# Letting token mixers in between the row tiles of the last layer's gate and branch products

## The chip, the core and the metric

One core of one Trainium2 chip runs the whole program, two layers of a trunk, as one launch. The metric is the device time of that launch in microseconds, the median of several runs. All times below are microseconds from the start of the span unless something else is said.

## What is computed

The reference is a two-layer trunk over 256 latent tokens and 256 context tokens of width 1024. In each layer one input projection feeds four mixers (a convolution module, a bidirectional state-space scan, a bidirectional retention, and a latent attention). What the mixers give is merged like this:

```
merged = sigmoid(gate_0) * (branch_0 @ w_branch[0])
for i in 1..3: merged += sigmoid(gate_i) * (branch_i @ w_branch[i])
out = merged @ w_out
```

Here gate_i is a 1024-wide part of the input projection `hx @ w_in`, and each branch is 512 wide. Then come an output projection with a residual, a norm and a SwiGLU. In the last layer only the 256 latent tokens go on, so the context tokens need no gates and no branch products there.

The convolution branch, the one that matters most below, is a 31-tap depthwise convolution, a layer norm over its 512 channels, and a SiLU.

## The kernel before, in words

All large products are made from a stream of weights: 128x128 blocks, eight to a chunk of 512 KB. Each chunk is loaded on the queue of SyncE, and then split into two parts, a rounded one (`whi`, one cast on ScalarE, L201) and the rest (`wlo`, two subtractions on VectorE, L268). A product of two such split operands is three matmuls (`mm3`). All matmuls have line L222 and all transposes L227, since both go through the helper `PE`.

**The order of the work** is set when the program is built. In each layer `lin` is a generator that gives out the products with `w_in`, the gates and the branch products. Beside it run the mixers, which are generators too: the scan, the latent attention and the retention go through one `stagger`, and the convolution stands "behind" them. `interleave` (L714) picks who goes on next. It keeps a clock of its own for each engine, from fixed prices per instruction (a 512-column matmul is width/2.4 + 13 ns), and its rules are:

- A mixer goes on if what it waits for is met by that clock, and VectorE's planned backlog is under a lead: 6 us for the three staggered mixers, 5 us for the convolution (`LEAD`, L41).
- If none may, `lin` goes on, up to its next `yield`. What `lin` gives out between two yields is one block, in which no mixer gets a place.
- A mixer says `yield at(t)` before a TensorE step that needs `t`, and is taken up again when the planner's TensorE clock has passed the time at which `t` is planned to be ready.

A mixer's matmul or transpose also gets a dependency on the last product that `lin` gave out before it (`PE._place`, L209), so that it can't be run sooner than its place in the program. It can be run later: the compiler's scheduler, which orders the instructions of each engine, may let later products of `lin` pass while the operand is not ready by its own estimate.

**The gates and branches of the last layer** are made by `rows` (L976), with the tokens as the stationary side and four weight blocks (128x512) as the moving side. I call one such 128x512 piece of a weight a row tile. For each of `nk` row tiles it runs `mm3` for two groups of 128 tokens, that is six matmuls of 512 columns, and it accumulates in two of the four banks tagged `mm`. A gate half has `nk` = 8 and so 48 matmuls, a branch half has `nk` = 4 and so 24. `gate_rows` (L987) makes four gate halves ahead, before any branch is needed (`GATES`, L49), and then one more ahead of each branch half, until all eight are done. The branches come in the order scan, latent attention, retention, convolution. In the trace the matmuls of `rows` are those with `whi` or `wlo` as the moving side, `mm<-whi,u` and `mm<-wlo,u`; those of all other large products are `mm<-u,whi` and `mm<-u,wlo`.

**The convolution** (L1566) gives out its 31 taps for two channel tiles at a time (VectorE, `u<-u,convw,u`). At its end it has a chain with four steps on TensorE: the sum over channels for the mean (`mx<-one,u`), the spread of the mean over the partitions (`mx<-cons,mean`), the transposes for the sum of squares (`mx<-cons,u`), and the spread of the reciprocal deviation (`mx<-cons,rs_y`). Between them VectorE subtracts, squares are made on ScalarE, and the reciprocal root is nine small VectorE instructions. After it the last branch's two halves can be made.

Other products of 256 tokens in the last layer (`win`, L852) have no yield inside them in this layer: the one at its fourth block (L860) is for 512 tokens alone, which is the first layer.

Of the kernel before, what the change touches and what calls it, by code (L numbers as in the profile page):

```python
# [19 lines left out]
KD = D // 128  # L20
# [32 lines left out]
OFF = {}  # L53
# [36 lines left out]
def ar(o, n=128):  # L90
    return np.arange(o, o + n)
# [90 lines left out]
def trunk(ctx: ExitStack, tc: tile.TileContext, xin: bass.AP, cin: bass.AP, par: bass.AP, con: bass.AP,  # L182
# [62 lines left out]
    def mm():  # L245
        return psm.tile([128, 512], F32, tag="mm", name=nm("mm"))

    def mx():
        t = psx.tile([128, 512], F32, tag="mx", name=nm("mx"))
        banks.append(t.tensor.name)  # L250
        return t
# [10 lines left out]
    def stt(o, i0, s, i1, op0, op1):  # L262
        spent("dve", o, (i0, i1), 70 + 1.14 * width(o))
        V.scalar_tensor_tensor(out=o, in0=i0, scalar=s, in1=i1, op0=op0, op1=op1)  # L264

    def tt(o, i0, i1, op):
        spent("dve", o, (i0, i1), 70 + 1.05 * width(o))
        V.tensor_tensor(out=o, in0=i0, in1=i1, op=op)  # L268
# [14 lines left out]
    def split(hi, lo, src, scale=None):  # L283

        if scale is None:
            A.copy(hi, src)
            tt(lo, src, hi.bitcast(F32), SUB)
        else:
            A.activation(hi, src, AF.Copy, scale=scale)
            stt(lo, src, scale, hi.bitcast(F32), MUL, SUB)  # L290

    def mm3(o, ah, al, bh, bl, start, stop):
        PE.matmul(o, ah, bh, start=start, stop=False, skip_group_check=True)
        PE.matmul(o, ah, bl, start=False, stop=False, skip_group_check=True)
        PE.matmul(o, al, bh, start=False, stop=stop, skip_group_check=True)
# [27 lines left out]
    @contextmanager  # L323
    def urgent():
        before, who["urgent"] = who["urgent"], True
        with tc.high_priority():
            yield
        who["urgent"] = before
# [87 lines left out]
    def w_ensure(chunk):  # L416
        while W["split"] <= min(chunk + W["ahead"], NCHUNK - 1):
            c = W["split"]
            w_load(c + W["load"])
            hi = wpool.tile([128, 1024], F32R, tag="whi", name=nm("whi"))  # L420
            lo = wpool.tile([128, 1024], F32R, tag="wlo", name=nm("wlo"))
            with urgent():
                raw_ = W["raw"].pop(c)
                A.copy(hi, raw_)
                for o_ in (0, 512):
                    tt(lo[:, o_:o_ + 512], raw_[:, o_:o_ + 512], hi[:, o_:o_ + 512].bitcast(F32), SUB)
            W["hl"][c] = (hi, lo)
            W["hl"].pop(c - 8, None)
            W["split"] += 1

    def w_take(blocks, align=1):

        W["pos"] = (W["pos"] + align - 1) // align * align
        pos = W["pos"]
        wlist.append((pos, blocks))
        W["pos"] += len(blocks)
        return pos

    def w_block(b, n=1):
        w_ensure(b // 8)  # L440
        hi, lo = W["hl"][b // 8]
        o = (b % 8) * 128
        return hi[:, o:o + 128 * n], lo[:, o:o + 128 * n]

    def linear(arr, nk, cols, X, N, k0=0, c0=0):

        pos = w_take([(arr, k0 + k, cols) for k in range(nk)])
        ps = mm()
        c = slice(c0, c0 + N)
        for k in range(nk):  # L450
            wh, wl = w_block(pos + k)
            mm3(ps[:, c], wh, wl, X[k][0][:, c], X[k][1][:, c], k == 0, k == nk - 1)
        return ps
# [5 lines left out]
    def linear_wide(arr, nk, cols, X, k0=0):  # L459

        pos = w_take([(arr, k0 + k, cols) for k in range(nk)])
        ps = mm()
        for k in range(nk):
            wh, wl = w_block(pos + k)
            wide_step(ps, wh, wl, X[k], k == 0, k == nk - 1)
        return ps[:, 0:SEQ], ps[:, SEQ:2 * SEQ]
# [212 lines left out]
    def stagger(units, wide):  # L679

        units, live = iter(units), []
        while True:
# [28 lines left out]
            if r is None:  # L711
                yield None

    def interleave(lin, others):  # L714


# [80 lines left out]
    hx = [None] * KD  # L797
# [20 lines left out]
    for l in range(L):  # L818
# [33 lines left out]
        def win(name, i, n):  # L852

            pos_ = w_take([(("w_in", l), k_, ar(OFF[name] + 128 * i)) for k_ in range(KD)])
            ps_ = mm()
            for k_ in range(KD):
                wh_, wl_ = w_block(pos_ + k_)
                mm3(ps_[:, :n], wh_, wl_, hx[k_][0][:, :n], hx[k_][1][:, :n], k_ == 0, k_ == KD - 1)
                if k_ == 3 and n == T:
                    yield None  # L860
            return ps_
# [21 lines left out]
        def lin():  # L883
# [42 lines left out]
            for i in range(4):  # L926
                pa = yield from win("conv", i, N)
                pg = yield from win("conv", 4 + i, N)
# [46 lines left out]

            def rows(arr, nk, o, X):  # L976

                pos_ = w_take([(arr, k_, ar(o + 128 * m_)) for k_ in range(nk) for m_ in range(4)], 4)
                pr_ = [mm() for _ in range(nb)]
                for k_ in range(nk):  # L980
                    wh_, wl_ = w_block(pos_ + 4 * k_, 4)
                    for b_ in range(nb):
                        bs_ = slice(b_ * 128, (b_ + 1) * 128)
                        mm3(pr_[b_], X[k_][0][:, bs_], X[k_][1][:, bs_], wh_, wl_, k_ == 0, k_ == nk - 1)
                return pr_

            def gate_rows(ahead):  # L987
                while todo and len(gates) < ahead:
                    i_, h_ = todo.popleft()
                    tl_ = []  # L990
                    for pg in rows(("w_in", l), KD, OFF["gate"] + 1024 * i_ + 512 * h_, hx):
                        t_ = U([128, 512])
                        A.activation(t_, pg, AF.Tanh, scale=0.5)
                        tl_.append(t_)
                    gates.append(tl_)
                    yield

            if last:
                todo = deque((i, h) for i in order for h in range(2))
                sums, mg = [None] * 2, []  # L1000
                yield from gate_rows(GATES[l])
                for n, i in enumerate(order):
                    yield f"br{i}"
                    bx = []
                    for t in br[i]:
                        hi, lo = U.pair(N)
                        split(hi[:, :N], lo[:, :N], t[:, :N], 0.5 if i in (0, 2) else None)
                        U.put(t)
                        bx.append((hi, lo))
                    for h in range(2):  # L1010
                        yield from gate_rows(GATES[l] + 1 if n < 3 else len(todo))
                        tl = gates.popleft()
                        pbs = rows(("w_branch", l, i), 4, 512 * h, bx)
                        with urgent():
                            for t, pb in zip(tl, pbs):
                                stt(t, t, 1.0, pb, ADD, MUL)
                            if n == 0:
                                sums[h] = tl
                            else:
                                for a_, t in zip(sums[h], tl):  # L1020
                                    tt(a_, a_, t, ADD)
                                    U.put(t)
                        if n == 3:
                            if h == 1:
                                U.put(hx)
                            for q in range(2):
                                p = mx()
                                for f2 in range(2):
                                    for b in range(nb):
                                        o = (2 * q + f2) * 128  # L1030
                                        PE.transpose(p[:, (2 * f2 + b) * 128:(2 * f2 + b + 1) * 128],
                                                     sums[h][b][:, o:o + 128], ident)
                                for f2 in range(2):
                                    mg.append(U.wide(SEQ))
                                    split(*mg[-1], p[:, SEQ * f2:SEQ * f2 + SEQ], 0.5)
                            U.put(sums[h])
                        yield None
                    U.put(bx)
                R["mo"] = mg
                return  # L1040

            yield from gate(GATES[l])
            for n, i in enumerate(order):
                yield f"br{i}"
                bx = []
# [627 lines left out]
        hx = out_by_stream(("w_out", l), mo, KD, 0, 16, (l, "n2g", 24))  # L1673
# [4 lines left out]
        for a, b in grp:  # L1678
# [29 lines left out]
            for j in range(j, b):  # L1708
                pa = linear_wide(fin, KD, ar(128 * j), hx) if last else linear(fin, KD, ar(128 * j), hx, N)
                filler()  # L1710
                pg = (linear_wide(fin, KD, ar(FFN + 128 * j), hx) if last else
                      linear(fin, KD, ar(FFN + 128 * j), hx, N))
# [15 lines left out]
        else:  # L1728
            hx = r
# [6 lines left out]
    for k in range(KD):  # L1736
        o, _ = PCOL["fing"]
# [136 lines left out]
```

## Time and profile before

| what | value |
|---|---|
| runs | 1690.01, 1684.65, 1690.13 us; median 1690.01 |
| profiled execution | 1687.63 us |
| its span | 1685.9 us, 24281 instructions |
| TensorE (PE) busy | 1631.7 us, 97% of the span |
| VectorE (DVE) busy | 1314.3 us, 78% |
| ScalarE (ACT) busy | 809.7 us, 48% |
| granted TensorE clock | 0.991 of full on average |

The profiled execution took 1.7 us more than its span, for what lies around it. "Busy" is the time in which an engine had an instruction; matmuls are pipelined and their ends are modelled, so neighbouring matmuls overlap in the rows, and the distance between starts tells how fast they really go. "Granted clock" is 1.00 for the 2.4 GHz level and 0.50 for the 1.2 GHz level; a value between is a mean over a stretch with both.

### The profile page before, as it was taken

How to read it: one execution, taken by the hardware profiler on the slowest of the kernel's cores; microseconds unless marked ns; L12 is line 12 of the kernel's file. 1: busy time of each engine (PE TensorE's matmuls, PEld its weight loads, DVE VectorE, ACT ScalarE, POOL GpSimd, SP SyncE). 2: the span in 40 equal slices, each digit the busy share in tenths (PEclk: the TensorE clock that was granted, in tenths of full speed). 3: DMA queues.
4: the chain of work that ended last, by engine and by line, in shares of the span. 5: the costliest groups of instructions: out<-in, count | busy, mean ns of one | idle time of the engine just before them, and what ended most of it. 6: DMA issues, size and time to landing. Idle time of an engine off the chain costs nothing.

```text
span 1685.9 us, 24281 instructions
## 1 busy us (share of the span) xinstructions
PE 1631.7 (97%) x8926; PEld 1357.7 (81%) x8926; DVE 1314.3 (78%) x2676; ACT 809.7 (48%) x1378; POOL 49.0 (3%) x89
## 2 busy tenths in 40 slices
PE   6999999999999999999999999999999998899997
PEld 4787776778878879988888889988788786778886
DVE  4879997689996577887657657679996987777765
ACT  3475579552243234423222335467659443455553
POOL 0010200000000000000000000000200000000000
PEclk9999999999999999999999999999999999899999
DMA  9344321215445445455456646446433467345564
GB/s 361 131 133 138 107 70 61 71 47 157 131 135 177 152 160 177 138 187 175 154 171 211 218 138 196 138 118 198 123 100 123 142 213 244 111 140 187 187 188 137
DMA packets 85096, 259.04 MB, mean 154 GB/s; under 512 B 9648, under 2 KB 18784, under 8 KB 84976
## 3 DMA queue, kind: packets, MB, share of 16 engines
q1 hardware_dynamic: 73584, 244.15, 45.3%
q10 hardware_dynamic: 10624, 12.28, 2.9%
q0 software_dynamic: 768, 1.05, 0.3%
q8 instruction: 70, 1.15, 0.3%
q14 instruction: 50, 0.41, 0.1%
HBM read 253.70 MB, written 2.18 MB: 152 GB/s over the span
## 4 chain that ended last, share of the span: by engine, by line
PE 85%; DVE 8%; ACT 3%; DMA 3%; issue 2%; POOL 0%; ACTq 0%; DVEq 0%; POOLq 0%
PE mm L222 73%; PE mx L222 9%; DVE u L264 3%; PE mx L227 3%; DVE wlo L268 2%; DMA u<-drow 2%; DVE u L268 2%; ACT u L196 1%; ACT whi L201 1%; DVE u L279 1%; POOL u L346 0%; ACT u L201 0%; DMA u<-xin 0%; DMA c_raw<-cin 0%; DVE rs_s L268 0%
## 5 line engine op out<-in xcount | busy, mean ns | idle before, releaser
L222 PE MATMUL mm<-u,whi 128*128 128x512 f32 (+1 forms) x4088 | 1149.5, 363 | 2.9 <-DVE u L264 1.8
L222 PEld LDWEIGHTS mm<-u,whi 128*128 128x128 f32 x4088 | 728.5, 190 | 125.6 <-issue 9.2
L222 PE MATMUL mm<-u,wlo 128*128 128x256 f32 (+1 forms) x2332 | 785.0, 337 | 0.4 <-DVE wlo L268 0.3
L201 ACT CAST whi<-raw 128x1024 fp32r<-128x1024 f32 x351 | 368.3, 1050 | 540.4 <-PE mm L222 346.8
L268 DVE TENSOR_TENSOR wlo<-raw,whi 128x512 fp32r<-128x512 f32 x702 | 462.7, 688 | 180.2 <-ACT whi L201 178.7
L222 PEld LDWEIGHTS mm<-u,wlo 128*128 128x128 f32 x2332 | 442.8, 190 | 46.9 <-issue 1.0
L196 ACT ACTIVATE u<-u 128x256 f32<-128x256 f32 (+6 forms) x262 | 122.8, 483 | 157.4 <-DVE u L268 108.9
L264 DVE SCALAR_TENSOR_TENSOR u<-raw,cs,u 128x512 f32<-128x512 f32 x210 | 147.4, 746 | 57.4 <-DMA raw<-w_ada 56.8
L222 PE MATMUL mm<-whi,u 128*128 128x512 f32 x544 | 175.0, 398 | 4.4 <-ACT u L196 4.4
L268 DVE TENSOR_TENSOR u<-u,u 128x512 f32<-128x512 f32 (+5 forms) x289 | 159.7, 571 | 14.7 <-ACT u L201 5.2
L264 DVE SCALAR_TENSOR_TENSOR u<-u,convw,u 128x253 f32<-128x253 f32 (+27 forms) x240 | 133.2, 599 | 0.0
L222 PEld LDWEIGHTS mm<-whi,u 128*128 128x128 f32 x544 | 102.5, 189 | 28.3 <-ACT u L196 6.2
L222 PE MATMUL mx<-u,u 128*64 128x256 f32 (+6 forms) x644 | 118.4, 387 | 2.1 <-ACT whi L201 1.0
L222 PE MATMUL mm<-wlo,u 128*128 128x512 f32 x272 | 106.8, 392 | 0.0
L222 PEld LDWEIGHTS mx<-u,u 128*64 128x64 f32 (+3 forms) x644 | 75.1, 162 | 37.0 <-issue 9.3
L196 ACT ACTIVATE u<-mm 128x512 f32<-128x512 f32 (+3 forms) x110 | 60.7, 552 | 36.6 <-PE mm L222 31.5
L346 POOL TENSOR_SCALAR_AFFINE_SELECT u<-u 128x256 f32<-128x256 f32 (+1 forms) x64 | 40.3, 630 | 1208.2 <-DVE u L279 938.6
L264 DVE SCALAR_TENSOR_TENSOR u<-u,mm 128x512 f32<-128x512 f32 (+1 forms) x94 | 60.1, 646 | 11.9 <-PE mm L222 11.5
L264 DVE SCALAR_TENSOR_TENSOR u<-u,u 128x256 f32<-128x256 f32 (+3 forms) x114 | 62.0, 551 | 8.9 <-ACT u L196 8.7
L222 PEld LDWEIGHTS mm<-wlo,u 128*128 128x128 f32 x272 | 51.5, 189 | 10.7 <-issue 0.7
L227 PE MATMUL mx<-cons,u 128*128 128x128 f32 (+1 forms) x292 | 45.0, 279 | 12.6 <-DVE u L268 10.7
L227 PEld LDWEIGHTS mx<-cons,u 128*128 128x128 f32 (+1 forms) x292 | 34.1, 143 | 25.5 <-issue 13.6
(113 smaller groups left out, 870.0 us busy)
## 6 DMA issues: line engine op xcount, KB each, us to landing
raw<-wst SPq DMA_DIRECT2D x354, 512.0 KB, 3.7
raw<-w_ada SPq DMA_DIRECT2D x72, 512.0 KB, 3.9
u<-wfirst SPq DMA_DIRECT2D x32, 256.0 KB, 6.4
u<-drow ACTq DMA_DIRECT2D x32, 256.0 KB, 4.7
u<-xin SPq DMA_DIRECT2D x16, 256.0 KB, 4.4
u<-w_ada SPq DMA_DIRECT2D x16, 256.0 KB, 4.3
u<-drow ACTq DMA_DIRECT2D x16, 128.0 KB, 4.5
spill<-u SPq DMA_DIRECT2D x8, 128.0 KB, 3.7
```

The lines of the kernel that those rows point to most:

```text
L196: nc.scalar.activation(o, i, *a, **k)
L201: nc.scalar.copy(o, i)
L222: PE._place(nc.tensor.matmul(o, a, b, **k))
L227: PE._place(nc.tensor.transpose(o, *a, **k))
L264: V.scalar_tensor_tensor(out=o, in0=i0, scalar=s, in1=i1, op0=op0, op1=op1)
L268: V.tensor_tensor(out=o, in0=i0, in1=i1, op=op)
L279: V.tensor_scalar(out=o, in0=i0, scalar1=s1, scalar2=s2, op0=op0, op1=op1)
L346: G.affine_select(out=out, in_=in_, **k)
```

## The change

`rows` becomes a generator. It takes its weight blocks from the stream four at a time, when it comes to their row tile, where it had taken all of them at its start. After each row tile but the last it yields, so that `interleave` may give a mixer a place there. Its two callers take its result with `yield from`. No instruction is added or removed in the source, and nothing outside the last layer's `rows` changes.

```
             def rows(arr, nk, o, X):
-                pos_ = w_take([(arr, k_, ar(o + 128 * m_)) for k_ in range(nk) for m_ in range(4)], 4)
                 pr_ = [mm() for _ in range(nb)]
                 for k_ in range(nk):
-                    wh_, wl_ = w_block(pos_ + 4 * k_, 4)
+                    wh_, wl_ = w_block(w_take([(arr, k_, ar(o + 128 * m_)) for m_ in range(4)], 4), 4)
                     for b_ in range(nb):
                         bs_ = slice(b_ * 128, (b_ + 1) * 128)
                         mm3(pr_[b_], X[k_][0][:, bs_], X[k_][1][:, bs_], wh_, wl_, k_ == 0, k_ == nk - 1)
+                    if k_ < nk - 1:
+                        yield None
                 return pr_

             def gate_rows(ahead):
...
-                    for pg in rows(("w_in", l), KD, OFF["gate"] + 1024 * i_ + 512 * h_, hx):
+                    for pg in (yield from rows(("w_in", l), KD, OFF["gate"] + 1024 * i_ + 512 * h_, hx)):
...
-                        pbs = rows(("w_branch", l, i), 4, 512 * h, bx)
+                        pbs = yield from rows(("w_branch", l, i), 4, 512 * h, bx)
```

## Rows read from the trace of the kernel before

**Rows 1.** The page: busy time of each engine over the span.
```profile
PE 1631.7 (97%) x8926; PEld 1357.7 (81%) x8926; DVE 1314.3 (78%) x2676; ACT 809.7 (48%) x1378; POOL 49.0 (3%) x89
```

**Rows 2.** Windows: stretch, length, busy us (instructions) by engine, clock, DMA share, GB/s.
```profile
275.00:525.00 250.00, 249.02 (x1175) 198.30 (x1174) 215.29 (x389) 116.32 (x190) 4.64 (x8) 1.00 0.36 114
1125.00:1275.00 150.00, 142.91 (x897) 121.59 (x896) 142.66 (x334) 102.11 (x209) 19.26 (x31) 0.99 0.45 133
1275.00:1424.00 149.00, 148.87 (x696) 120.58 (x696) 119.26 (x257) 83.13 (x127) 4.56 (x8) 1.00 0.60 191
1424.00:1437.10 13.10, 1.32 (x4) 0.58 (x4) 9.76 (x28) 5.08 (x12) 0.00 (x0) 0.59 0.38 122
```

**Rows 3.** The chain of waits from 1360 to 1437: start, us, what.
```profile
1369.26 37.65 PE mm L222 x166
1406.92 0.34 PE mx L222 x4
1407.26 5.61 PE mm L222 x24
1412.86 0.22 PE mx L227 x2
1413.08 9.63 PE mm L222 x43
```

**Rows 4.** Timeline of TensorE from 1423 to 1440; in brackets idle before and releaser.
```profile
1429.02 0.66 PE L227 MATMUL mx<-cons,u 128*128 128x128 f32 x2 [5.04 <-DVE u L268]
1432.27 0.66 PE L227 MATMUL mx<-cons,rs_y 128*128 128x128 f32 x2 [2.59 <-DVE rs_y L264]
1437.14 0.80 PE L222 MATMUL mm<-whi,u 128*128 128x512 f32 x1 [4.21 <-ACT u L196]
...
1440.19 0.39 PE L222 MATMUL mm<-wlo,u 128*128 128x512 f32 x1
```

**Rows 5.** Timeline of VectorE from 1365 to 1369: the last tap and the sum behind it.
```profile
1365.89 0.47 DVE L264 SCALAR_TENSOR_TENSOR u<-u,convw,u 128x241 f32<-128x241 f32 x1
...
1367.56 0.42 DVE L268 TENSOR_TENSOR u<-u,u 128x256 f32<-128x256 f32 x1
```

**Rows 6.** Windows of the same form: where VectorE has room.
```profile
1275.00:1300.00 25.00, 25.00 (x133) 20.07 (x134) 14.40 (x30) 22.79 (x44) 2.02 (x4) 1.00 0.46 146
1300.00:1366.00 66.00, 65.90 (x305) 52.98 (x304) 62.65 (x151) 33.69 (x52) 2.53 (x4) 1.00 0.49 152
1377.00:1424.00 47.00, 46.98 (x210) 38.55 (x209) 31.85 (x55) 21.02 (x24) 0.00 (x0) 1.00 0.83 261
```

**Rows 7.** The chain of waits: one whole gate half; then its two neighbours of mixer work.
```profile
1292.95 1.31 PE mx L227 x12
...
1294.69 10.89 PE mm L222 x48
1305.58 2.52 PE mx L222 x18
```

**Rows 8.** Groups of TensorE from 1275 to 1424: the two largest of eight.
```profile
L222 PE MATMUL mm<-whi,u 128*128 128x512 f32 x352 | 111.5, 393 | 0.0
L222 PE MATMUL mm<-wlo,u 128*128 128x512 f32 x176 | 68.6, 390 | 0.0
```

**Rows 9.** Timeline of TensorE inside the first gate half: mixer products between its matmuls.
```profile
1278.14 0.39 PE L222 MATMUL mm<-wlo,u 128*128 128x512 f32 x1
1278.37 1.32 PE L222 MATMUL mx<-u,u 96*128 96x512 f32 x5
...
1280.42 0.63 PE L222 MATMUL mm<-whi,u 128*128 128x512 f32 x2
```

**Rows 10.** A hole in front of a mixer's transposes (timeline), and windows around it.
```profile
1151.90 0.63 PE L227 MATMUL mx<-cons,u 128*128 128x128 f32 x4 [3.40 <-DVE u L268]
...
1152.00:1156.00 4.00, 4.00 (x25) 4.00 (x26) 4.00 (x8) 3.33 (x8) 0.00 (x0) 0.67 0.62 158
1156.00:1160.00 4.00, 4.00 (x33) 4.00 (x32) 3.38 (x9) 1.97 (x3) 0.00 (x0) 0.90 0.61 198
```

More of the change, by code (lines that the diff above doesn't have):

```diff
@@ L976, in rows @@
             def rows(arr, nk, o, X):
-                pos_ = w_take([(arr, k_, ar(o + 128 * m_)) for k_ in range(nk) for m_ in range(4)], 4)
                 pr_ = [mm() for _ in range(nb)]
                 for k_ in range(nk):
-                    wh_, wl_ = w_block(pos_ + 4 * k_, 4)
+                    wh_, wl_ = w_block(w_take([(arr, k_, ar(o + 128 * m_)) for m_ in range(4)], 4), 4)
                     for b_ in range(nb):
@@ L984, in rows @@
                         mm3(pr_[b_], X[k_][0][:, bs_], X[k_][1][:, bs_], wh_, wl_, k_ == 0, k_ == nk - 1)
+                    if k_ < nk - 1:
+                        yield None
                 return pr_
@@ L990, in gate_rows @@
                     tl_ = []
-                    for pg in rows(("w_in", l), KD, OFF["gate"] + 1024 * i_ + 512 * h_, hx):
+                    for pg in (yield from rows(("w_in", l), KD, OFF["gate"] + 1024 * i_ + 512 * h_, hx)):
                         t_ = U([128, 512])
@@ L1012, in lin @@
                         tl = gates.popleft()
-                        pbs = rows(("w_branch", l, i), 4, 512 * h, bx)
+                        pbs = yield from rows(("w_branch", l, i), 4, 512 * h, bx)
                         with urgent():
```

## The prediction

> **What bounds the kernel.** The busy times come first: TensorE has work for 97% of the span, VectorE for 78% [rows 1]. So time can only be won where TensorE stands, and I next looked for holes, stretch by stretch, in the last layer's mixing stage. The windows show three kinds [rows 2]. From 1275 to 1424, where all eight gate halves and six of the eight branch halves run, TensorE is idle for 149.00 - 148.87 = 0.13 us. From 1125 to 1275, before the first gate, it is idle for 7.1 us, but nothing of the change lies there. From 1424.0 to 1437.1 it has work for 1.32 us of 13.10, and the granted clock falls to 0.59 on average. That is the hole to be explained.
>
> The timeline of TensorE tells what it waits for [rows 4]: the transposes for the sum of squares (5.04 us), the spread of the deviation (2.59 us), and the first matmul of the last branch (4.21 us), each released by VectorE or ScalarE. These are the last steps of the convolution's closing chain. Nothing is left to cover them, since all gates and all other branches are used up.
>
> Why is that chain late? Its last tap ran at 1365.89 and the sum over channel tiles that the mean needs was done at 1367.56 + 0.42 = 1367.98 [rows 5]. But the product for the mean ran at 1406.92 in the chain of waits, behind 166 matmuls of `rows` in one piece [rows 3]. Its operand lay ready for 38.9 us. It could not run sooner, as 166 is the rest of one gate half, then branch, gate, branch, gate (22 + 24 + 48 + 24 + 48), and a mixer has its place only between such blocks. The next step, the spread of the mean, ran at 1412.86, again exactly one block (24) later. VectorE is not what holds the chain there: between 1377 and 1424 it has work for 31.85 us of 47 [rows 6]. So the end of this stage is set by the places that the planner gave the chain.
>
> **The change part by part.**
>
> *What stays.* The 384 matmuls of the gates and 192 of the branches are the same; up to 1424 the groups show 352 + 176 = 528 of them, and the other 48 are the last branch [rows 8]. Casts, splits and weight loads follow the order of the blocks. Taking four blocks at a time instead of 32 or 16 would reorder the stream only if a mixer took weights in between, and no group of a product with streamed weights other than `rows` is among the eight of that stretch [rows 8]. So SyncE's queue gets the same loads in the same order, at no cost. The two accumulating banks stay open longer; no one else asks for such a bank there.
>
> *What moves.* A block of `lin` shrinks from 48 or 24 matmuls to six. A gate half is 10.89 us for 48, so 0.227 us each [rows 7], and a row tile is 6 x 0.227 = 1.36 us. Two things follow for the chain. First, a step whose operand is planned ready inside a block waits 1.36 us at most, not 10.89 or 5.45. Secondly, the taps themselves get earlier places. The planner lets the convolution go on only while VectorE's planned backlog is under 5 us, and then gives out a whole gate half; 10.89 - 5 = 5.9 us of each such half is VectorE time that it plans as idle. With a question after each row tile it refills every 1.36 us. Seven more gate halves lie between the first one and the mean's product; where the staggered mixers have no work ready, the convolution is the one that fills VectorE. If only two of the seven give back their 5.9 us, that is 11.8 us, and the mean's own wait for the end of the gate half before it adds on average half a block, 5.4 us. I count on 17 us or more.
>
> *What is needed.* Once started, the chain took from 1406.92 to 1437.14, that is 30.2 us, with one block of waiting in it [rows 3, 4]. If it starts 13.1 us sooner, at 1393.8, it is done when the other work of TensorE ends, and the hole is gone. If it started when its operand was ready, it would be done at 1367.98 + 30.2 = 1398.2, 26 us early. Between 13.1 needed, 17 expected and 38.9 possible, I take the hole as closed. The cover is the work that is left: 9.63 us of the two retention halves behind the spread of the mean, and the gates before them [rows 3].
>
> *What that gives.* The three waits: 5.04 + 2.59 + 4.21 = 11.84 us [rows 4]. The first matmuls after the hole ran at the lower level: seven starts from 1437.14 to 1440.19 took 3.05 us where seven at 0.227 take 1.59, so 1.46 us more [rows 4, 7]. The four transposes took 2 x 0.66 us there and take about 0.5 us less at full clock (four with 0.63 us in all stand in another row, though behind a hole too [rows 10]). Together 13.8 us.
>
> *What it may cost.* More mixer products stand between row tiles, and each may be a little late. The trace of before doesn't show these places, so I bound it: 0.13 us as in the gates' stretch now, 7.1 us as in the stretch before it, where `lin` goes in steps of under 3 us and mixers are densest. Below nothing it can't be, as there is no idle time left to win. The nearest row is the first layer's stage with finer steps, 250.00 - 249.02 = 0.98 us [rows 2]. I take 1.0.
>
> *Does breaking a run of matmuls cost by itself?* In the first gate half mixer products already stand between its matmuls: five of them at 1278.37, the next `rows` matmul at 1280.42 with no idle time, at a granted clock of 1.00 [rows 6, 9]. So I count nothing for it. The Trainium skill ("Perfetto Trace Analysis", section "Matmul Optimizations") says the opposite in tendency: matmuls should be issued back to back in batches, since the engine's power follows how much it is used. By that rule the change is wrong, and the sum would be that of the last rival below. The trace agrees with the rule where holes are real [rows 10], and not where only other matmuls come between [rows 9].
>
> **Sum.** 13.8 - 1.0 = 12.8 us less. The profiled execution took 1687.63, so 1674.8; it lies 2.4 us below the median of the runs and 3.0 above the lowest, and from the median the same sum gives 1677.2. I say 1676. About 0.5%, 8.4 us, is what a measurement of this kernel can tell from no change.
>
> **The rivals.**
>
> *Half closed.* The chain moves by one block or so and not by 13 us. For it: VectorE has work for 62.65 of 66 us up to the last tap [rows 6], so the taps can hardly be done sooner, and the chain would then share VectorE with weight splits. Against it: the 38.9 us of lying ready come after that. A move by half of what is needed leaves half the hole: 13.8/2 - 1.0 = 5.9 us less, 1682 to 1684.
>
> *The places don't decide.* The compiler's scheduler puts a mixer's product behind later products when it thinks the operand is late; it did so inside the first gate half [rows 9]. If its estimate for the mean's operand, and not the planner's place, kept the product back until 1406.92, then the change doesn't do what it says, and the time stays at 1687 to 1690. Against it: the mean's product and the next step stand exactly at block ends.
>
> *Slower: holes at row tiles.* Place: the retention and scan work of 1275 to 1366, where VectorE is full [rows 6]. A mixer's product that now gets its place 5 to 9 us sooner is not yet fed, the compile-time estimate misses that, and TensorE stands, with all row tiles behind it. Price: the hole at 1148 is such a one, 3.40 us idle, then the clock at 0.67 and 0.90 for 4 us each, which loses 4 x 0.33 + 4 x 0.10 = 1.7 us [rows 10]; 5.1 us in all. Three of them eat the gain; for slower by over 8.4 us it takes (13.8 + 8.4)/5.1, five of them, and then 1687.6 - 13.8 + 25.5 = 1699. For it: five late ones are within reach, as 696 - 528 = 168 matmuls from 1275 to 1424 are the mixers' [rows 2, 8]. Against it: the 0.13 us of now, with products already between row tiles, and the 0.98 us of the first layer at fine steps [rows 2].
>
> **How the numbers follow.** Hole closed: 0.66, time 1671 to 1680. Half closed: 0.13. Places don't decide: 0.11. Slower or near it by holes: 0.10. Faster by over 0.5% takes the first case and a third of the second, 0.70. Same takes the rest of the second, the third and the milder part of the last, 0.20. Slower: 0.10. The range must take in no change, up to 1690, and at the low end the lowest of the runs less the whole 13.8 us, 1671; with 2 us of room below that I give 1669 to 1690. For the likeliest case alone it is 1671 to 1680.
>
> **What would show it.** In the profile of the changed kernel the `mx<-one,u` product should stand between row tiles, between 1370 and 1394, with `mx<-cons,mean`, the transposes and `mx<-cons,rs_y` following well before the last retention half is done. The window of 13 us with 1.32 us of TensorE work should be gone, and the first matmul of the last branch should follow the one before without a wait and at clock 1.00. The groups of `rows` should have the same counts. It would be wrong if the hole is there as before, with the mean's product no more than one block sooner, or if new waits of several microseconds on VectorE or ScalarE stand in front of mixer products between 1275 and 1366.

## The result, and the profile after

The changed kernel takes 1677.82 us (median of 10 runs, 1674.11 to 1682.40), the kernel before, measured beside it, 1689.66 (10 runs, 1684.65 to 1699.52). That is 11.8 us less. The ratio is 0.9937, with a 95% interval of 0.9923 to 0.9951: 8 to 13 us less. The profiled execution took 1674.50, span 1672.8, which is 13.1 us less than that of before. It is **faster**, by 0.6%, and the interval excludes a ratio of 1; the sum that was forecast is 12.8 us.

The page shows the same number of instructions on every engine and nearly the same busy time [rows 1]. Nothing was taken out. TensorE's idle time fell by 10.4 us (1685.9 - 1631.7 = 54.2 before, 1672.8 - 1629.0 = 43.8 now), and its busy time by 2.7.

```profile
PE 1629.0 (97%) x8926; PEld 1355.5 (81%) x8926; DVE 1314.7 (79%) x2676; ACT 810.6 (48%) x1378; POOL 50.8 (3%) x89
```

The windows that answer to [rows 2], in the same columns. The last 13.10 us, which held 1.32 us of TensorE work at clock 0.59, are now full at clock 1.00. In return the gates' stretch has 1.98 us of idle time instead of 0.13, and its clock is 0.98.

```profile
1275.00:1424.00 149.00, 147.02 (x672) 118.14 (x671) 121.39 (x270) 86.08 (x136) 5.94 (x8) 0.98 0.57 185
1424.00:1437.10 13.10, 13.10 (x62) 10.64 (x61) 11.56 (x19) 4.90 (x5) 0.00 (x0) 1.00 0.64 220
```

The chain of waits, where [rows 3] showed 166 `rows` matmuls in one piece in front of the mean's product (start, us, what):

```profile
1354.89 4.76 PE mm L222 x21
1359.65 0.34 PE mx L222 x4
1359.99 1.51 PE mm L222 x6
...
1373.67 61.45 PE mm L222 x271
```

And the timeline of TensorE, the four steps of the convolution's closing chain alone. None of them has a bracket: TensorE waited for none. Compare [rows 4], where the last two waited 5.04 and 2.59 us.

```profile
1359.49 0.50 PE L222 MATMUL mx<-one,u 128*128 128x1 f32 x4
...
1361.34 0.38 PE L227 MATMUL mx<-cons,mean 128*128 128x128 f32 x2
...
1368.63 0.41 PE L227 MATMUL mx<-cons,u 128*128 128x128 f32 x2
...
1373.26 0.40 PE L227 MATMUL mx<-cons,rs_y 128*128 128x128 f32 x2
```

In the chain of waits the mean's product starts at 1359.65 instead of 1406.92 [rows 3], and after the chain's last step on TensorE 271 `rows` matmuls follow in one piece, 61 us of them. Before, only the last branch came behind it, after a wait of 4.21 us [rows 4].

One thing is new. In front of a retention product TensorE now waits 1.83 us, and the twelve matmuls of that product take 4.44 us, where twelve of the same shape five us earlier took 2.10 (timeline):

```profile
1295.12 2.10 PE L222 MATMUL mx<-u,u 64*128 64x256 f32 x12
...
1300.19 4.44 PE L222 MATMUL mx<-u,u 64*128 64x256 f32 x12 [1.83 <-DVE u L264]
```

The windows around it (the clock is the third number from the end) show 0.77, 0.50 and 0.88:

```profile
1298.00:1302.00 4.00, 2.17 (x9) 1.63 (x8) 3.87 (x10) 3.21 (x7) 1.36 (x2) 0.77 0.44 131
1302.00:1306.00 4.00, 4.00 (x12) 2.69 (x9) 2.94 (x7) 1.21 (x4) 0.00 (x0) 0.50 0.01 2
1306.00:1310.00 4.00, 4.00 (x18) 3.40 (x17) 3.13 (x8) 1.79 (x4) 0.00 (x0) 0.88 0.19 35
```

### The profile page after: what moved, and what is told of

Same layout as the page of the kernel before. It is cut to its first block, busy times and chain, and to the rows that moved or that the text cites. A ratio compares the mean times of both kernels' runs of the same rounds, so it can differ in the third digit from the quotient of the medians.

```text
span 1672.8 us, 24292 instructions
## 1 busy us (share of the span) xinstructions
PE 1629.0 (97%) x8926; PEld 1355.5 (81%) x8926; DVE 1314.7 (79%) x2676; ACT 810.6 (48%) x1378; POOL 50.8 (3%) x89
## 4 chain that ended last, share of the span: by engine, by line
PE 85%; DVE 7%; DMA 3%; ACT 2%; issue 2%; POOL 0%; ACTq 0%; DVEq 0%; POOLq 0%; SPq 0%
PE mm L222 73%; PE mx L222 9%; DVE u L264 3%; PE mx L227 2%; DMA u<-drow 2%; DVE wlo L268 2%; DVE u L268 1%; ACT u L196 1%; ACT whi L201 1%; DVE u L279 1%; POOL u L346 0%; ACT u L201 0%; DMA u<-xin 0%; DMA raw<-wst 0%; DMA c_raw<-cin 0%
## 5 line engine op out<-in xcount | busy, mean ns | idle before, releaser
L268 DVE TENSOR_TENSOR u<-u,u 128x512 f32<-128x512 f32 (+5 forms) x289 | 159.9, 572 | 11.8 <-ACT u L201 5.3
L264 DVE SCALAR_TENSOR_TENSOR u<-u,convw,u 128x250 f32<-128x250 f32 (+27 forms) x240 | 133.7, 598 | 0.0
L201 ACT COPY u<-mx 128x512 f32<-128x512 f32 (+4 forms) x82 | 37.4, 500 | 39.4 <-PE mx L222 38.2
```

The lines of the kernel that those rows point to most:

```text
L201: nc.scalar.copy(o, i)
```

## The experiments

What was to be told apart: does the gain come from the place of the convolution's closing chain, as forecast, or from something else that the yields do; is the interruption needed for it; and what does the new wait cost? Executions start their work some microseconds apart, so stages are compared by their length, from the transposes behind the hole of [rows 10] to the end of the last `rows` matmul: 298.7 us before, 288.2 after. One thing in these lengths is not the work of the kernels: the clock just behind that hole. It fell in the profile of before and stayed up in that of the changed kernel (windows, before and then after; the clock is the third number from the end):

```profile
1150.00:1162.00 12.00, 10.10 (x72) 10.13 (x73) 11.02 (x22) 7.79 (x17) 0.61 (x1) 0.86 0.63 198
...
1150.00:1162.00 12.00, 10.48 (x88) 10.51 (x89) 11.72 (x26) 8.83 (x17) 0.23 (x1) 1.00 0.70 195
```

That is 12 x 0.14 = 1.7 us of the 10.5 between the two lengths. In `e3` below this clock is 0.86, as before.

**Yields in the branch halves only** (`e1`).

```
-                    if k_ < nk - 1:
+                    if k_ < nk - 1 and nk == 4:
```

> Yields stay in the branch halves alone; gate halves are whole blocks of 48 again. If the place of the convolution's closing chain decides (theory): the chain's mean product still stands behind the eighth gate half, because its operand is planned ready inside gate blocks, and only the step behind it moves up by some 18 matmuls (4 us). A hole of 5 to 10 us in front of the last branch stays, time 1682 to 1690. If any six-matmul step in rows is what helps (rival): the hole is gone and the time is that of the changed kernel, 1674 to 1682.

Measured: 0.9982 [0.9972, 0.9993], 1687.13 us. The timeline of TensorE, the chain's steps and the first matmul of the last branch:

```profile
1410.55 0.50 PE L222 MATMUL mx<-one,u 128*128 128x1 f32 x4
...
1412.40 0.38 PE L227 MATMUL mx<-cons,mean 128*128 128x128 f32 x2
...
1426.50 0.41 PE L227 MATMUL mx<-cons,u 128*128 128x128 f32 x2
...
1433.67 0.66 PE L227 MATMUL mx<-cons,rs_y 128*128 128x128 f32 x2 [5.59 <-DVE rs_y L264]
...
1438.53 0.80 PE L222 MATMUL mm<-whi,u 128*128 128x512 f32 x1 [4.21 <-ACT u L196]
```

The mean's product stays where it was, with 120 `rows` matmuls behind it in both traces, and the hole with it: 5.59 + 4.21 = 9.8 us of the 11.84 remain. The gates' yields carry the gain. With yields in the gates alone the program has the same instructions in the same order as the changed kernel, on every engine; behind such gates the mixers have nothing left to put between a branch's row tiles.

**A long lead for the convolution from the stage's start, no yields** (`e2`). The planner lets the convolution run until VectorE's planned backlog is 16 us instead of 5, in the last layer; `rows` is that of before.

```
+LEAD1 = (6e3, 16e3)
...
-... ahead < LEAD[w_ == conv] ...
+... ahead < (LEAD if l == 0 else LEAD1)[w_ == conv] ...
```

> The kernel before with no yield in rows, but in the last layer the planner lets the convolution go on while VectorE's planned backlog is under 16 us instead of 5 us, so that it is given its taps and its closing chain early. Theory (the chain's place decides, not the interruption): mean product and the three steps behind it stand well before the last branch, the 13 us hole is gone, 1674 to 1682. Rival (it is the finer interleaving of all mixers with the gate products that helps): no gain, 1685 to 1692. Second risk under the theory: the other mixers now wait for VectorE behind the taps, and new holes of some us each show before 1275.

Measured: 1.0046 [1.003, 1.0061], 1696.72 us: slower, and outside both ranges. The last window is full, but the stretches before it are not; the two largest groups of TensorE's waits from 1100 to 1424 (us in total, times, longest) name VectorE (line numbers are two higher in this kernel):

```profile
1100.00:1275.00 175.00, 163.38 (x945) 142.74 (x944) 161.87 (x383) 88.78 (x153) 8.44 (x13) 0.97 0.50 146
1275.00:1424.00 149.00, 138.47 (x682) 106.72 (x681) 108.17 (x257) 105.85 (x211) 16.70 (x27) 0.95 0.45 129
1424.00:1437.00 13.00, 13.00 (x59) 10.75 (x58) 7.74 (x13) 5.90 (x7) 0.00 (x0) 1.00 0.74 241
```

```profile
PE mm L224 <- DVE u L270: 7.9, 2, 7.4
PE mx L229 <- DVE rs_y L266: 5.2, 2, 3.3
```

The taps come first (the last starts at 1259.2, where it was 1365.9), and TensorE then waits for other work of VectorE: 175.00 - 163.38 = 11.6 us idle before the gates' stretch, where some 7 were there before [rows 2], and 10.5 in it. The stage takes 307.2 us. So an early chain by itself is not a gain; it has to be early at the cost of nothing that TensorE waits for.

**The first four gate halves whole, yields from the fifth on** (`e3`, and again as `e10`).

```
-                    if k_ < nk - 1:
+                    if k_ < nk - 1 and len(todo) < 4:
```

> The first four gate halves (made before any branch) are whole again, the later four gate halves and the branches yield after every row tile. Theory: the chain's four steps get places among the later gate halves, with about 90 matmuls of rows (21 us) left behind the last of them, so the 13 us hole is gone. The new wait of 1.8 us in front of a retention product at 1300, which stands among the first gate halves of the changed kernel, is gone too: idle from 1275 to the last branch under 0.5 us. Time 1672 to 1681. Rival (early mixing work must be interrupted for the gain): the hole stays at 5 us or more, 1682 to 1690.

Measured: 0.9890 [0.9877, 0.9903], 1671.83 us. Windows, and two places of the timeline:

```profile
1275.00:1424.00 149.00, 148.67 (x697) 120.43 (x696) 125.44 (x282) 87.28 (x140) 4.55 (x8) 1.00 0.58 188
1424.00:1437.00 13.00, 13.00 (x63) 10.46 (x61) 11.74 (x21) 6.07 (x9) 0.00 (x0) 1.00 0.80 241
```

```profile
1322.78 4.58 PE L222 MATMUL mx<-u,u 64*128 64x256 f32 x20
...
1387.15 0.50 PE L222 MATMUL mx<-one,u 128*128 128x1 f32 x4
```

The hole is closed though the mean's product runs at 1387.15, 28 us later than in the changed kernel, and the wait of 1.83 us is gone: the retention's twelve matmuls stand in a run of twenty at 1322.78, which takes 0.229 us each. Idle in the gates' stretch: 0.33 us. The stage takes 284.9 us, 298.7 - 284.9 = 13.8 less than before. The taps are not earlier here: the last starts at 1371.7, 6 us later than before. What is shorter is the time for which the mean's operand lies ready, from 1374.1 on, 13 us.

**Products of the output projection as cover behind the branches** (`e4`). The changed kernel, with the first halves of four products of `w_out` given out around the transposes of the second half's merge.

```
+ def first_half(fs_): # wide_step(..., mg[k_], k_ == 0, False) for k_ in range(4), per f_
...
+ if h == 1:
+     first_half(range(2) if q == 0 else [2])
...
+ if h == 1:
+     first_half([3])
```

> The changed kernel, and besides the products of the output projection that need only the first half of the merged channels (32 matmuls, about 5.6 us) are given out around the transposes of the second half instead of all behind them. Theory: the two waits behind the last branch, 0.93 and 1.30 us, and four pairs of matmuls at the lower clock behind them (1.3 us) go, 2 to 3.5 us less than the changed kernel: 1671 to 1678 and its idle time from 1437 to 1451 under 0.5 us. Rival (the splits of the second half are then late instead): the same wait moves in front of the products of the second half, no gain.

Measured: 0.9934 [0.9916, 0.9951], 1680.23 us: above the range, and no gain over the change. The timeline shows the waits still there, in front of the merge's transposes:

```profile
1449.40 0.30 PE L227 MATMUL mx<-cons,u 128*128 128x128 f32 x1 [0.96 <-DVE u L268]
...
1451.12 0.55 PE L227 MATMUL mx<-cons,u 128*128 128x128 f32 x3 [1.06 <-DVE u L268]
```

In front of the first wait stand four matmuls of those products, as many as in the changed kernel, and in front of the second two more; the rest came behind. So this cover was hardly ever in front of the waits, and whether it would help there wasn't settled.

**The long lead only once four gates are out, no yields** (`e5`).

```
-... ahead < LEAD[w_ == conv] ...
+... ahead < (LEAD1 if who.get("long") else LEAD)[w_ == conv] ...
...
                         yield from gate_rows(GATES[l])
+                        who["long"] = True
```

> The kernel before with no yield in rows; the planner's lead for the convolution is 16 us instead of 5 us, but only once the first four gate halves are given out, so that the other mixers have nearly all their VectorE work before it. Theory (the place of the closing chain decides, whatever gives it that place): all four steps stand at ends of whole blocks, the last with one gate half's worth of rows matmuls (about 11 us) behind it; the 13 us hole is gone and none of the holes of the 16 us lead from the start come; stage from the 3.4 us hole to the end of rows 284 to 289 us where the kernel before took 298.7, time 1670 to 1680. Rival (the chain must be interrupted into blocks to run early without harm): the hole stays at 4 us or more or as much idle comes elsewhere, 1682 to 1692.

Measured: 0.9924 [0.9910, 0.9937], 1676.63 us, the gain of the change with not one product interrupted. The stage takes 288.7 us. In the timeline the mean's product stands at 1391.62, with 192 `rows` matmuls behind it instead of 120, and a smaller wait inside the last branch is left (line numbers are two higher again); it wasn't followed up.

```profile
1391.62 0.61 PE L224 MATMUL mx<-one,u 128*128 128x1 f32 x4
...
1430.55 0.96 PE L224 MATMUL mm<-whi,u 128*128 128x512 f32 x3 [2.19 <-DVE u L266]
```

**One yield, in the middle of each of the last four gate halves** (`e6`).

```
-                    if k_ < nk - 1:
+                    if k_ == 3 and nk == KD and len(todo) < 4:
```

> Only the later four gate halves yield, and only once, in their middle; the branches and the first four gate halves are whole. Theory: blocks of 24 matmuls (5.4 us) are fine enough; the chain's last step stands with some 66 matmuls (15 us) of rows behind it, the hole is gone, same time as with the first four whole and a yield after every row tile, 1669 to 1675. If the step of six matmuls matters: a hole of some us in front of the last branch, 1676 to 1684.

Measured: 0.9920 [0.9907, 0.9933], 1674.19 us. Four yields in place of dozens give the gain of the change, but a part of the rival came true too: a wait inside the last branch is left, and the clock fell behind it (timeline, then windows).

```profile
1431.99 1.65 PE L222 MATMUL mm<-whi,u 128*128 128x512 f32 x3 [1.74 <-DVE u L264]
```

```profile
1432.00:1436.00 4.00, 4.00 (x12) 3.23 (x13) 0.94 (x3) 0.58 (x2) 0.00 (x0) 0.64 0.55 188
```

The stage takes 289.2 us, 4.3 more than in `e3`.

**All of `e3`, but the chain held back** (`e7`) until the last retention half is given out.

```
+            if ns == 1:
+                yield "cover"
             m = sm([128, 1, nb], "mean")
...
+                    if n == 3:
+                        yield "+cover"
```

> The kernel with the first four gate halves whole and all later blocks of six matmuls, but the convolution's closing chain may start only when the last retention half is given out, so that nothing covers it. All interruptions stay. Theory: TensorE stands for the chain's whole length, 13 to 18 us with some 1.5 us of its own work in it, plus about 2 us at the lower clock: 1685 to 1693, as slow as the kernel before or slower. Rival (the finer interleaving gives the gain): 1669 to 1676, unchanged.

Measured: 1.0006 [0.9996, 1.0017], 1690.27 us: the gain is gone whole. The timeline has the four waits of the chain, 3.13 + 2.99 + 2.59 + 4.21 = 12.9 us:

```profile
1427.49 0.50 PE L222 MATMUL mx<-one,u 128*128 128x1 f32 x4
...
1431.12 0.69 PE L227 MATMUL mx<-cons,mean 128*128 128x128 f32 x2 [3.13 <-DVE mean L277]
...
1434.80 0.66 PE L227 MATMUL mx<-cons,u 128*128 128x128 f32 x2 [2.99 <-DVE u L268]
...
1438.05 0.66 PE L227 MATMUL mx<-cons,rs_y 128*128 128x128 f32 x2 [2.59 <-DVE rs_y L264]
...
1442.92 0.80 PE L222 MATMUL mm<-whi,u 128*128 128x512 f32 x1 [4.21 <-ACT u L196]
```

**Yields in the first four gate halves only** (`e8`, the condition `len(todo) >= 4`).

> Only the first four gate halves yield after each row tile; the later four and the branches are whole. Theory: the chain's last step stands with about 190 matmuls (43 us) behind it, so the 13 us hole is gone; but the wait of 1.8 us in front of a retention product at 1300 and the low clock behind it stay as in the changed kernel, since its place is among the first four: stage from the 3.4 us hole to the end of rows 287 to 290 us, time 1674 to 1682, above the version with the first four whole. Rival (the wait at 1300 was chance): as fast as that version, 1669 to 1674.

Measured: 0.9932 [0.9919, 0.9944], 1677.33 us. The hole is closed (the mean's product ran 66.5 us before the last branch's first matmul: 1362.1 and 1428.6), the stage takes 289.5 us, and the new wait is there, with the low clock behind it (groups of waits from 1155 on, then windows):

```profile
PE mx L222 <- DVE u L264: 2.0, 1, 2.0
```

```profile
1302.00:1306.00 4.00, 4.00 (x11) 2.75 (x9) 2.96 (x7) 1.46 (x4) 0.00 (x0) 0.50 0.01 2
```

So either half of the gates closes the hole, and only yields in the first four bring the new wait.

**The changed kernel and `e3` on one chip** (`e9`, `e10`), for what that wait is worth.

> The changed kernel once more, beside the next one on the same chip: ratio to the kernel before 0.992 to 0.995, and again a wait of 1.8 to 2.5 us in front of a retention product near 1300 with the lower clock behind it.

> The version with the first four gate halves whole once more. If the interruptions of the first four cost what the profiles show (3.3 us from the 3.4 us hole to the end of rows), its ratio is 0.0015 to 0.005 below that of the changed kernel beside it, 0.988 to 0.992; if the first result was a lucky chip or run, the two ratios are within 0.001 of each other.

Measured: 0.9940 [0.9926, 0.9954], 1677.90 us, for the changed kernel (six runs, 1672.98 to 1679.60), and 0.9908 [0.9893, 0.9923], 1671.69, for the other (five, 1670.71 to 1674.84). The intervals lie just apart, as those of `e3` and of the first measurement do: **keeping the first four gate halves whole beats the change**, by some 0.3%. In the profile of `e9`, however, the same wait had another consequence (timeline, then windows):

```profile
1302.16 2.65 PE L222 MATMUL mx<-u,u 64*128 64x256 f32 x12 [1.83 <-DVE u L264]
```

```profile
1298.00:1302.00 4.00, 2.33 (x14) 1.45 (x12) 4.00 (x8) 4.00 (x8) 2.48 (x4) 1.00 0.28 99
1302.00:1306.00 4.00, 3.84 (x17) 3.07 (x18) 4.00 (x13) 2.75 (x8) 0.00 (x0) 1.00 0.20 77
```

The clock stayed at 1.00. That profiled execution took 1672.98, the shortest of its six, at a mean clock of 0.997; the other five took 1675.89 to 1679.60 at 0.993 to 0.995. So the wait was as expected, and the lower clock behind it was not there.

## Why the prediction was right, and where it was not

**The hole and its size: right.** The sum put the three waits, the slow matmuls behind them and the slow transposes at 13.8 us. `e3`, in which nothing else is lost, shortens the stage by 13.8, with the same clock of 0.86 at the stage's start as before. The window is full and the four steps have their cover, as was said; only the place differs, as the mean's product runs at 1359.5 and not between 1370 and 1394.

**The sum: near, in part by chance.** The forecast was 12.8 us; the medians differ by 11.8 and the profiled executions by 13.1. But in the profiles the change has lost more than the 1.0 us of the sum: 1.85 us of idle time and 3.4 us of clock (below), which would leave 13.8 - 5.2 = 8.6. That the stage is nonetheless 10.5 us shorter is for the most part due to the 1.7 us of clock at its start, and the other 2.6 us of the 13.1 lie outside the stage, where the change does nothing. For `e3`, too, 3.2 of the 17.0 us between the profiles lie there. What sets them is open.

**The cause, the chain's place among the products: right, and shown.** `e7` has all of `e3`'s yields with the chain late, and is where the kernel before was; `e5` has no yield with the chain early, and has the gain. So the rival by which the places don't decide is excluded, and the yield is only one way to give the place. Neither dozens of yields (`e6`, but for a wait of 1.74 us) nor those of the branches (`e1`, and the program that is the same without them) are needed.

**Why the chain had its late place: only in part right.** "It could not run sooner" doesn't follow from 166 = 22 + 24 + 48 + 24 + 48: within those matmuls four blocks end, and at each of these ends the planner passed the product over. So the wait for the end of a block can't be all of the 38.9 us. The planner's own clock, read while the program is built, has the operand ready 8.9 us before the product gets its place; for the rest of the 38.9 us the operand was ready on the chip and not yet by that clock.

**How the chain got earlier: more than counted on, and by another road.** The text counted on 17 us or more, from shorter waits for a place and from the planner's 5.9 us per gate half. Measured: the mean's product moved by 47 us, more even than the 38.9 that were called possible. For half of that the taps account: the last of them starts at 1342.4 (the group's own row, VectorE) instead of 1365.89 [rows 5].

```profile
L264 DVE SCALAR_TENSOR_TENSOR u<-u,convw,u x120: 444/468/714, 1188.0 to 1342.4; 128x255 f32<-128x255 f32 x8, 128x254 f32<-128x254 f32 x8, 128x253 f32<-128x253 f32 x8, 128x252 f32<-128x252 f32 x8
```

The half-closed rival held that to be impossible, since VectorE was full up to the last tap [rows 6]. It was full, but not of mixer work alone. The stretch from the first gate to the last tap, before and then after, first all engines, then VectorE's `wlo` splits (in the column of busy time):

```profile
1275.00:1366.00 91.00, 90.90 (x436) 73.05 (x437) 77.06 (x180) 56.48 (x94) 4.56 (x8) 1.00 0.48 151
...
1275.00:1366.00 91.00, 30.62 (x47) 1.00 0.48 151
```

```profile
1273.00:1343.00 70.00, 68.13 (x325) 53.31 (x324) 65.59 (x161) 46.54 (x85) 5.94 (x8) 0.95 0.33 108
...
1273.00:1343.00 70.00, 18.50 (x28) 0.95 0.33 108
```

The stretch is 21 us shorter: 30.62 - 18.50 = 12.1 us of splits now come behind the taps, and VectorE's idle time fell from 91.00 - 77.06 = 13.9 to 4.4 us. TensorE's groups of the same two stretches say the same, before:

```profile
L222 PE MATMUL mm<-whi,u 128*128 128x512 f32 x188 | 60.4, 396 | 0.0
L222 PE MATMUL mm<-wlo,u 128*128 128x512 f32 x94 | 36.7, 391 | 0.0
```

and after:

```profile
L222 PE MATMUL mm<-whi,u 128*128 128x512 f32 x108 | 36.5, 407 | 0.0
L222 PE MATMUL mm<-wlo,u 128*128 128x512 f32 x54 | 22.0, 408 | 0.0
```

Instead of 282 gate and branch matmuls only 162 ran by the last tap. The mixers get TensorE and VectorE more often at the start, and the products kept back are the cover later. The prediction saw the idle part of this (5.9 us per half), not that weight splits would make room. Earlier taps aren't needed for the gain, however: in `e3` they are later than before, and the hole is closed by the shorter wait for a place alone.

**"A step whose operand is planned ready inside a block waits 1.36 us at most": true of the plan, not of the chip.** After the last tap, VectorE's timeline has the sums that the mean needs:

```profile
1344.69 1.42 DVE L268 TENSOR_TENSOR u<-u,u 128x256 f32<-128x256 f32 x4
```

They are done by 1346.11 at the latest, and the product ran at 1359.49: 13.4 us, with only `rows` matmuls between. That is less than the 38.9 of before, but ten times the bound. The compiler's scheduler is not the cause: 342 `rows` matmuls stand behind the product in the trace, 57 whole row tiles, and 342 were left when the planner gave it out. By the planner's clock it came 0.7 us after its operand was ready. So the bound held there, and the 13.4 us arise because the planner has the work of VectorE later, against the matmuls, than the chip ran it. It cost nothing, as 61 us of `rows` matmuls were still to come behind the chain's last step.

**The cost of late mixer products: mis-sized.** The forecast took 1.0 us between bounds of 0.13 and 7.1. Idle time in the gates' stretch measures 1.98 - 0.13 = 1.85 us more than before, nearly all of it the one wait of 1.83 at 1300.19. To that comes the clock, for which the term had nothing: at 0.77, 0.50 and 0.88 for 4 us each, up to 4 x (0.23 + 0.50 + 0.12) = 3.4 us. So one late product costs an estimated 1.8 us where the clock holds (`e9`) and about 5 where it doesn't. It is the slower rival's mechanism, in the stretch and near the price that it named (5.1 us each), but one hole and not five. That its price changes from one execution to the next would fit the wider scatter of the changed kernel (1674.11 to 1682.40; `e3` and `e10` together 1670.63 to 1674.84) and a part of the 6 us between the medians of `e9` and `e10`. It is not shown to be all of it: the one profiled execution of the changed kernel with the low clock here took 1674.50, the second shortest of its ten, so the slower ones lost more than that, and where was not seen.

**Breaking a run of matmuls: nothing, as said.** In `e3` yields stand after every six matmuls of half the gates, with 0.33 us of idle time and a clock of 1.00 in the gates' stretch. The advice of the Trainium skill ("Perfetto Trace Analysis", section "Matmul Optimizations") to issue matmuls back to back in batches agrees with the trace behind some real holes (0.50 behind the wait at 1300) and not behind all (1.00 in `e9`), and there is no sign of it where another matmul takes the place.

## What to carry to other kernels

When the last thing to finish is a chain of small steps between big products, look for how long its operands lay ready: a lever that moves the chain's first step, with enough big products kept back to cover the rest, is worth most of the hole, and it may be a yield or a lead. Give such places late, where the chain needs them, and not from the start: places given too early here put a product of another mixer at a point where its operand wasn't there yet. And count the blocks that a ready operand lies through: if it is more than one, the plan's idea of when it is ready is late, not only its blocks long. A full engine is no proof that its work can't come sooner, as long as part of what fills it belongs to products that may wait.

## What was not expected of the hardware

A hole of only 1.83 us was followed by a granted clock of 0.50, the 1.2 GHz level, over all of the 4 us from 1302 on in one profile of the changed kernel, and by 1.00 throughout in another, with the same instruction waiting for the same releaser. The first row's twelve f32 matmuls then took 4.44 us, the second's 2.65, and without a hole they take 2.10. In `e8` the clock fell too, behind 2.0 us of the same wait. The longer hole of 3.40 us at the start of the stage has the same two outcomes: 0.86 over the 12 us around its end before, 1.00 in the changed kernel. What differs between the executions is open.
